# A norm's column products and root rows dealt out between other products, squares summed in three views, and T1 and T2 placed behind the blocks

## The chip, the cores and the metric

The kernel runs on one core of a Trainium2 chip. The metric is the device time of one launch in microseconds (us), the median of the runs. Engines are called as in the profile: PE is TensorE (matrix products), PEld its weight loads, DVE VectorE, ACT ScalarE, POOL GpSimd, SP SyncE (which starts DMAs here).

## What is computed

Two layers on a sequence of 1024 rows of 1024 numbers. Each has a token mixer (layer 0 forgetting attention, layer 1 gated linear attention, GLA) and a dense SwiGLU feed-forward part. Each of the four parts begins with an RMS norm, scaled and shifted by a conditioning vector:

```python
def rms_norm(x, g):
    y = x * rsqrt(mean(x * x, axis=-1, keepdims=True) + EPS)
    return y * g

for i in range(2):
    sh1, sc1, g1, sh2, sc2, g2 = split(silu(c) @ ada_w[i] + ada_b[i], 6)
    h = rms_norm(x, norm1_g[i]) * (1 + sc1) + sh1
    x = x + g1 * (attention(h) if i == 0 else gla(h))
    h = rms_norm(x, norm2_g[i]) * (1 + sc2) + sh2
    gate, up = split(h @ ffn_w_in[i], 2)
    x = x + g2 * ((silu(gate) * up) @ ffn_w_out[i])
return rms_norm(x, final_g)
```

All is float32. The change concerns the norm ahead of the two feed-forward parts and the norm between the layers.

## The kernel before

The activations lie transposed: x is eight tiles `xs[0..7]` of 128 features by 1024 rows, worked on in two halves of 512 rows (`hf` 0 and 1). To keep float32 precision, each factor is split into a high part (cast on ACT, L163) and a low part (subtraction on DVE, L164), and `mm3` (L240) makes three products for each tile of the contraction, high by high (L241), high by low (L242), low by high (L243). They add up in a bank of PSUM.

A norm of a half goes in these steps:

- `SumSq` (L572) squares the tile of each finished feature block m on ACT and adds squares on DVE and POOL (L590) in a tree. With `late=7` the last squares are not added in: four views remain (`roots`, L578), v0, v4, v6 and v7.
- `rms_cols` (L526) sums over the features: for each of four groups of 128 rows and each view, PE makes a product of 128x1 (L531) with a column of ones. These 16 are the column products, into the PSUM tile sp.
- DVE takes mean plus eps (L534), POOL the power -1/2 (L535), into rs.
- `rms_rows` (L539) spreads the result over all partitions by four products of 128x128 with the identity (L543), into rb: the rows.
- The views are scaled by rb and split: for the layer norm in `norm_half` (L549, te and h1h/h1l from L556 on), for the feed-forward part in `second_half` (L1209). There the feed-forward input is kept in blocks of the Strassen kind: B11 and B21 are the first half's, B12 and B22 the second half's (scaling at L1175, low part at L1183), T1 = B12 - B11 and T2 = B22 - B21 are differences (L1217 to L1220; low part of T1 at L1180).

While the second half is normed, PE has work of the first half: in the feed-forward stage the tiles (0,0), (0,1) and then (1,0) of gate and up, each of 8 x 3 products with 512 columns (`plain_tile`, L1330; PSUM tiles p); at the boundary between the layers the value products of GLA (`gv_body`, PSUM tiles gv, 256 columns each), with a split of the small weights w2t and aw on DVE.

The order on an engine is set by a scheduler that simulates a timeline of the program, and by `tc.issue_after(ins)`, which holds what is written in its block behind `ins` in the order only. Each engine runs its own list strictly in this order; waits between engines follow from the data. In before, the columns stand in the program ahead of the first tiles, the scheduler puts one of the 16 between the first products and the other 15 in one burst, and `GK = (2, 6)` holds products k >= 2 of tile (0,1) behind the columns, and those of k >= 6 behind the rows. At the boundary `sp_ins` and `rb_ins` do that for the second value body and the gate products.

The last stretch that the prediction speaks of is the first head of GLA: at00 and at01 are its score tiles (both in PSUM bank b3), atz the masked scores (copy on DVE, L1759), ahl their split, go the products with the values, gr the gate projection, kv the state products.

Of the kernel before, what the change touches and what calls it, by code (L numbers as in the profile page):

```python
# [9 lines left out]
F32 = mybir.dt.float32  # L10
# [4 lines left out]
ALU = mybir.AluOpType  # L15

P = 128
# [36 lines left out]
def trunk(ctx, tc, x, c, ada_w, ada_b, norm1_g, norm2_g, ffn_w_in, ffn_w_out,  # L54
# [171 lines left out]
    class Weights:  # L226
# [7 lines left out]
        def next(self):  # L234
# [2 lines left out]
                self.got.append(f(*a))  # L237
            return self.got.popleft()

    def mm3(ps, ah, al, bh, bl, start, stop):  # L240
        nc.tensor.matmul(ps, ah, bh, start=start, stop=False)  # L241
        nc.tensor.matmul(ps, ah, bl, start=False, stop=False)  # L242
        nc.tensor.matmul(ps, al, bh, start=False, stop=stop)  # L243

    def proj(ps, w, hs, hf):

# [273 lines left out]

    sp_ins, rb_ins = [], []
    LATE1 = 7
    GK = (2, 6)
    SPM, RBM = (3, 4)

    def rms_cols(ss, nm, psr, n=4):  # L526
# [17 lines left out]
        rb_ins.append(last_ins())  # L544
        return rb

    first_half = []

    def norm_half(xs, ss, hs, l, hf, psr, tmp):  # L549

        rb = rms_rows(ss, f"{l}0{hf}", psr)
        gates = [(SPM, sp_ins[-1]), (RBM, last_ins())]
        cs = hsl(hf)
        for k in range(8):
            y = tmp()
            hi, lo = hs[k].hi[:, cs], hs[k].lo[:, cs]  # L556
            if k % 2 == 0:
                nc.vector.scalar_tensor_tensor(y, xs[k][:, cs], acol(l, 0, k), rb, op0=ALU.mult, op1=ALU.mult)
                nc.scalar.activation(hi, y, AF.Identity, bias=mcol(l, 0, k))
                nc.vector.scalar_tensor_tensor(lo, y, mcol(l, 0, k), hi.bitcast(F32),  # L560
                                               op0=ALU.add, op1=ALU.subtract)
            else:
                nc.vector.tensor_mul(y, xs[k][:, cs], rb)
                nc.scalar.activation(y, y, AF.Identity, scale=acol(l, 0, k), bias=mcol(l, 0, k))
                nc.scalar.copy(hi, y)
                nc.gpsimd.tensor_sub(lo, y, hi.bitcast(F32))
        if hf == 0:
            first_half.append(last_of("G"))
        return gates

    class SumSq:


        def __init__(self, v, hf, late):
            w = slice(256 * (hf % 2), 256 * (hf % 2) + 256) if hf > 1 else slice(0, HALF)
            self.v = [v[i][:, w] for i in ((1, 3, 2, 5, 7, 6, 3, 4) if hf else range(8))]
            self.late = late
            self.roots = {0: [self.v[0]], 8: [self.v[0]], 7: [self.v[0], self.v[4], self.v[6], self.v[7]],  # L578
                          5: [self.v[0], self.v[4], self.v[5], self.v[6], self.v[7]]}[self.late]

        def __call__(self, m, xk):
            v = self.v
            nc.scalar.activation(v[m], xk, AF.Square)
            if self.late == 0:
                if m:
                    nc.vector.tensor_add(v[0], v[0], v[m])
                return
            d = 1
            while m & d and m < self.late:
                (nc.gpsimd if d == 1 and m < 4 else nc.vector).tensor_add(v[m - 2 * d + 1], v[m - 2 * d + 1], v[m - d + 1])  # L590
                d *= 2


    fr = deque(fl)
# [545 lines left out]
    def ffn(l, oh, xs, slots, nm, mid, norm_end, each=None):  # L1140
# [55 lines left out]
        last_chunk(4, 4, oh, xs, l, 2, nm, sv, norm)  # L1196
        dump(f"xa{l}", xs)
        sg = opr_["sg"]
        rb = rms_rows(ss1[0], f"{l}11", psr)
        block("B22", H_SL[0:4])  # L1200
        block("B12", H_SL[4:8])
        block("T1", H_SL[8:12])
# [3 lines left out]
        y12, y22 = yv_[:4], yv_[4:]  # L1206
        y11, y21 = ya[:4], ya[4:]

        def second_half():  # L1209
# [6 lines left out]
            for k in range(4):  # L1216
                nc.gpsimd.tensor_sub(y11[k], y12[k], y11[k])  # L1217
                split_t(T1[k], y11[k])
                nc.vector.tensor_sub(y11[k], y22[k], y11[k])
                split_t(T2[k], y11[k], sh(k + 4))  # L1220

        x_sp = tc.dram_tile([8, P, S], F32, name=f"x_sp{l}")
        for k in range(8):
# [100 lines left out]

        pin = Ring(psp, list(pj.q) + list(psr.q))
        gs = [Group(*g) for g in GROUPS]
        second_half()
        wgs = [[[None, None], [None, None]] for _ in range(2)]

        def plain_tile(kind, m, hf, after=()):  # L1330
            wg = wgs[kind]
            ps = pin([P, HALF], F32, f"p{l}")
            for k in range(8):
# [5 lines left out]
                with ExitStack() as es:  # L1339
                    for k_, ins in after:  # L1340
                        if k >= k_:
                            es.enter_context(tc.issue_after(ins))
                    mm3(ps, w.hi[:, k % 4, :], w.lo[:, k % 4, :], hi(t), lo(t), k == 0, k == 7)
            d = gate_view(0, (m, hf))
            if kind == 0:
                nc.scalar.activation(d, ps, AF.Silu)
# [1 line left out]
            nc.vector.tensor_mul(d, d, ps)  # L1348
            hid_done(0, (m, hf))

        plain_tile(0, 0, 0)
        plain_tile(0, 1, 0, ((GK[0], sp_ins[-1]), (GK[1], rb_ins[-1])))
        plain_tile(1, 0, 0, ((0, rb_ins[-1]),))
# [494 lines left out]
    with tc.issue_after(sp_ins[-1]):  # L1848
        vt.append(gv_body(0, wv, 1))
    with tc.issue_after(rb_ins[-1]):  # L1850
        bt = gate_tiles(0)
        a_body(aw, 0, bt)
# [125 lines left out]
```

## Time and profile before

| | |
|---|---|
| runs | 2413.99, 2417.68, 2418.18 us; median 2417.68 us |
| span of the profiled execution | 2415.5 us (the page gives no other time of it) |
| mean granted PE clock | 0.993 |
| PE products | 12342 records |
| DMA | 361.88 MB, mean 150 GB/s |

A row of a timeline is: start, duration, engine, line, operation, output<-inputs, shapes, count, and in brackets the idle time before it and what ended that. Times are us from the start of the span. Matmuls are pipelined: a 512-column product is shown with 0.39 us, though one starts every 0.23. The granted clock is a share of full speed, by stretch.

### The profile page before, as it was taken

What the parts mean: (1) busy time and instruction counts of PE and PEld (TensorE: products, weight loads), DVE (VectorE), ACT (ScalarE), POOL (GpSimd) and SP (SyncE); (2) the same over time, 40 slices, a digit from 0 to 9 for tenths busy, and PEclk for the clock granted to TensorE, in tenths of its full rate; (3) what the DMA queues carried; (4) which work ended last, traced back from release to release, by engine and by line L of the source; (5) the groups of instructions that cost most, each with busy time, mean ns of one, the idle gap of its engine ahead of it and who ended that gap; (6) DMA issues with size and microseconds to landing.
All of it is one profiled execution on the core that took longest, in us unless ns stands there. A gap on an engine that the chain in (4) does not pass through costs nothing.

```text
span 2415.5 us, 36053 instructions
## 1 busy us (share of the span) xinstructions
PE 2373.4 (98%) x12342; PEld 2018.3 (84%) x12342; DVE 1672.9 (69%) x2789; ACT 1191.8 (49%) x2288; POOL 1203.4 (50%) x1071
## 2 busy tenths in 40 slices
PE   7999999999999999999999999999999999999998
PEld 6788888878888888888888888898888888888888
DVE  6577677676687877876787545435586767675787
ACT  4665555675544444445324856654343333345325
POOL 4343344432347878853263646662335656653262
PEclk9999999999999999999999999999999999999999
DMA  9233333123335555457665334434325444347664
GB/s 272 72 106 114 100 111 105 62 97 114 127 103 178 184 172 174 155 187 260 228 201 171 89 110 126 135 124 154 114 85 172 164 133 151 133 174 256 232 202 148
DMA packets 329359, 361.88 MB, mean 150 GB/s; under 512 B 24460, under 2 KB 252968, under 8 KB 329176
## 3 DMA queue, kind: packets, MB, share of 16 engines
q1 hardware_dynamic: 328984, 359.57, 45.4%
q8 instruction: 97, 1.59, 0.3%
q14 instruction: 86, 0.70, 0.1%
q10 hardware_dynamic: 192, 0.02, 0.0%
HBM read 269.25 MB, written 90.24 MB: 149 GB/s over the span
## 4 chain that ended last, share of the span: by engine, by line
PE 82%; DVE 5%; DMA 4%; ACT 3%; issue 2%; POOL 2%; SPq 1%; DVEq 0%; POOLq 0%; ACTq 0%
PE p_b L243 16%; PE p_b L241 16%; PE p_b L242 16%; PE o_b L979 2%; PE t_b L965 2%; PE qk_b L241 2%; PE qk_b L243 2%; PE qk_b L242 2%; PE s_b L934 1%; PE s_b L935 1%; PE gr_b L243 1%; PE gr_b L242 1%; PE gr_b L241 1%; PE vps_b L241 1%; PE vps_b L242 1%
## 5 line engine op out<-in xcount | busy, mean ns | idle before, releaser
L164 DVE TENSOR_TENSOR o_s<-xv_s,o_s 128x512 fp32r<-128x512 f32 (+1 forms) x376 | 341.4, 911 | 78.4 <-ACT o_s L163 77.5
L163 ACT CAST o_s<-xv_s 128x512 fp32r<-128x512 f32 (+1 forms) x376 | 217.8, 587 | 320.3 <-PE p_b L243 254.4
L242 PE MATMUL p_b<-B,o_s 128*128 128x512 f32 x608 | 238.1, 392 | 0.0
L243 PE MATMUL p_b<-B,o_s 128*128 128x512 f32 x608 | 237.7, 391 | 0.0
L241 PE MATMUL p_b<-B,o_s 128*128 128x512 f32 x608 | 236.2, 391 | 0.0
L945 POOL TENSOR_SCALAR lp_s<-lp_s,st 128x128 f32<-128x128 f32 (+7 forms) x128 | 98.1, 771 | 265.7 <-DVE st L944 214.7
L708 POOL TENSOR_TENSOR ex_s<-xv_s,xv_s 128x512 f32<-128x512 f32 (+1 forms) x64 | 89.1, 1393 | 261.5 <-DMA xv_s<-in_ffn_w_in_dram 97.1
L241 PE MATMUL p_b<-T,o_s 128*128 128x512 f32 x480 | 186.7, 389 | 0.0
L242 PE MATMUL p_b<-T,o_s 128*128 128x512 f32 x480 | 186.7, 389 | 0.0
L243 PE MATMUL p_b<-T,o_s 128*128 128x512 f32 x480 | 180.7, 389 | 0.0
L243 PEld LDWEIGHTS p_b<-B,o_s 128*128 128x128 f32 x608 | 114.7, 189 | 23.9
L241 PEld LDWEIGHTS p_b<-B,o_s 128*128 128x128 f32 x608 | 114.7, 189 | 23.8
L242 PEld LDWEIGHTS p_b<-B,o_s 128*128 128x128 f32 x608 | 114.7, 189 | 23.7
L943 ACT ACTIVATE lp_s<-lp_s,st 128x128 f32<-128x128 f32 (+7 forms) x128 | 99.3, 777 | 61.1 <-DVE st L939 58.7
L381 POOL TENSOR_TENSOR ad_s<-ad_s,ad_s 128x512 f32<-128x512 f32 x62 | 89.4, 1442 | 54.0 <-ACT ad_s L379 29.6
L163 ACT CAST pt_s<-t_b 128x512 fp32r<-128x512 f32 (+1 forms) x160 | 79.6, 547 | 73.5 <-PE t_b L965 72.8
L710 POOL TENSOR_TENSOR xv_s<-ex_s,xv_s 128x512 f32<-128x512 f32 (+1 forms) x64 | 84.9, 1327 | 57.3 <-DVE o_s L164 55.1
L1319 DVE TENSOR_TENSOR ex_s<-ex_s,p_b 128x512 f32<-128x512 f32 x140 | 94.0, 680 | 27.0 <-PE p_b L243 26.9
L164 DVE TENSOR_TENSOR pt_s<-t_b,pt_s 128x512 fp32r<-128x512 f32 (+1 forms) x160 | 96.8, 631 | 13.2 <-ACT pt_s L163 12.9
L243 PEld LDWEIGHTS p_b<-T,o_s 128*128 128x128 f32 x480 | 90.1, 188 | 18.7
L241 PEld LDWEIGHTS p_b<-T,o_s 128*128 128x128 f32 x480 | 90.1, 188 | 18.7
L242 PEld LDWEIGHTS p_b<-T,o_s 128*128 128x128 f32 x480 | 90.1, 188 | 18.7
(1952 smaller groups left out, 7505.7 us busy)
## 6 DMA issues: line engine op xcount, KB each, us to landing
xv_s<-in_ffn_w_in_dram SPq DMA_DIRECT2D x176, 256.0 KB, 3.0
hid_B<-x SPq DMA_DIRECT2D x70, 512.0 KB, 2.7
ad_s<-in_ada_w_dram SPq DMA_DIRECT2D x384, 64.0 KB, 1.9
hid_T<-x SPq DMA_DIRECT2D x36, 512.0 KB, 2.8
xv_s<-in_ffn_w_out_dram SPq DMA_DIRECT2D x96, 192.0 KB, 4.1
ada_s<-in_ada_w_dram SPq DMA_DIRECT2D x128, 128.0 KB, 2.6
xv_s<-in_ffn_w_out_dram SPq DMA_DIRECT2D x40, 256.0 KB, 2.8
T2o<-hid_T SPq DMA_DIRECT2D x18, 512.0 KB, 9.0
```

The source lines that it names most:

```text
L163: nc.scalar.copy(hi, src)
L164: nc.vector.tensor_sub(lo, src, hi.bitcast(F32))
L241: nc.tensor.matmul(ps, ah, bh, start=start, stop=False)
L242: nc.tensor.matmul(ps, ah, bl, start=False, stop=False)
L243: nc.tensor.matmul(ps, al, bh, start=False, stop=stop)
L381: nc.gpsimd.tensor_add(acc, acc, raw)
L708: nc.gpsimd.tensor_add(s1, a21, a22)
L710: nc.gpsimd.tensor_sub(a11, s1, a11)
L943: nc.scalar.activation(lp, lp, AF.Exp, bias=mcur, scale=-1.0, accum_out=st[:, qi, 2:3])
L945: nc.gpsimd.tensor_scalar(lp, lp, st[:, qi, 3:4], 1.0, op0=ALU.mult, op1=ALU.mult)
L965: nc.tensor.transpose(tp[:, i, :], lps[qi][:, psl(2 * b + jj)], ident)
L1319: nc.vector.tensor_add(d, d if src is None else dest(G, src), ps)
```

## The change

Three edits, for the second half's norms with `late=7` (the first feed-forward stage, the boundary, and the second feed-forward stage):

1. *Three views.* After the square of m = 5, DVE adds v4 to v0 (L647 of after), and `roots` has three entries. A norm has 12 column products.
2. *Dealing.* `rms_later` returns the norm's steps as functions: the four columns of v0; then four pairs of the other two views, the root, a number of empty steps (8, or 13 at the boundary), and the four rows one by one. They go into the list `between`. Each product of `mm3` now takes one step from it and places it behind itself, and the next product behind the step. In the feed-forward stage v0's columns start at k = 4 of tile (0,0) and the rest at k = 2 of tile (0,1). At the boundary 24 empty steps, then v0's columns, belong to the first value body, the rest to the second.
3. *T1 and T2.* The step that makes T1 and T2 is held behind the last DVE instruction of B22.

The core of the diff:

```diff
+    def product(ps, a, b, start, stop):
+        with ExitStack() as es:
+            if tail:
+                es.enter_context(tc.issue_after(tail.pop()))
+            nc.tensor.matmul(ps, a, b, start=start, stop=stop)
+        if between:
+            f = between.popleft()
+            with tc.issue_after(last_of("P")):
+                if f is not None:
+                    f()
+            tail.append(last_of("P"))
...
-        nc.tensor.matmul(ps, ah, bh, start=start, stop=False)
+        product(ps, ah, bh, start, False)
...
-    GK = (2, 6)
+    GK = 2
...
+    def rms_later(ss, nm, psr, then, gap=8):
...
+        return ([lambda t=t: sums(0, t) for t in range(4)],
+                [lambda t=t: last(t) for t in range(4)] + [root] + [None] * gap
+                + [lambda t=t: row(t) for t in range(4)])
...
-            self.roots = {0: [self.v[0]], 8: [self.v[0]], 7: [self.v[0], self.v[4], self.v[6], self.v[7]],
+            self.roots = {0: [self.v[0]], 8: [self.v[0]], 7: [self.v[0], self.v[6], self.v[7]],
...
+            if self.late == 7 and m == 5:
+                nc.vector.tensor_add(v[0], v[0], v[4])
...
+            with tc.issue_after(last_of("D")):
+                for k in range(4):
+                    nc.gpsimd.tensor_sub(y11[k], y12[k], y11[k])
+                    split_t(T1[k], y11[k])
...
+        small = rms_later(ss1[0], f"{l}11", psr, second_half)
+        plain_tile(0, 0, 0, 4, small[0])
+        plain_tile(0, 1, 0, GK, small[1])
+        with tc.issue_after(rb_ins[-1]):
+            plain_tile(1, 0, 0)
...
+    between.extend([None] * 24 + second_norm[0])
     vt = [gv_body(0, wv, 0)]
+    between.extend(second_norm[1])
+    vt.append(gv_body(0, wv, 1))
```

The lists of the engines show what moves. PE in the first feed-forward stage, before; p0 are the tiles, sp011 the columns, and the views are ss0_s31 (v0), s34 (v4), s32 and s33:

```order
L242 MATMUL p0_b4_1_7662<-B2103_7116,o00001_s20_2_7456 128x512
L243 MATMUL p0_b4_1_7662<-B2103_7116,o00001_s20_2_7456 128x512
L531 MATMUL sp011_b6_3_7489<-ones_74,ss0_s34_7108 128x1
L531 MATMUL sp011_b6_3_7489<-ones_74,ss0_s32_7106 128x1
L531 MATMUL sp011_b6_3_7489<-ones_74,ss0_s33_7107 128x1
L531 MATMUL sp011_b6_3_7489<-ones_74,ss0_s31_7105 128x1
```

PE at the same norm, after, from the last products with B11 on:

```order
L247 MATMUL p0_b4_1_7590<-B1103_7112,o00000_s19_1_7422 128x512 x3
L247 MATMUL p0_b4_1_7590<-B2100_7113,o00001_s20_2_7457 128x512
L569 MATMUL sp011_b6_3_7607<-ones_74,ss0_s31_7105 128x1
L247 MATMUL p0_b4_1_7590<-B2100_7113,o00001_s20_2_7457 128x512
L569 MATMUL sp011_b6_3_7607<-ones_74,ss0_s31_7105 128x1
L247 MATMUL p0_b4_1_7590<-B2100_7113,o00001_s20_2_7457 128x512
```

The burst began behind the tile's last product; v0's columns now begin in the middle of the tile, behind its 20th product in the list (tile (0,1)'s first ones, which stand among them, counted in). DVE there, after; x0 are the updates of x, L644 is the add of square 5, L647 the new one:

```order
L1130 SCALAR_TENSOR_TENSOR x0_6_6212<-fo1461p_b2_15_7460,modc_167,x0_6_6212 128x512
L1130 SCALAR_TENSOR_TENSOR x0_7_6213<-fo1471p_b3_16_7475,modc_167,x0_7_6213 128x512
L644 TENSOR_TENSOR ss0_s34_7108<-ss0_s34_7108 128x512
L647 TENSOR_TENSOR ss0_s31_7105<-ss0_s31_7105,ss0_s34_7108 128x512
L578 TENSOR_SCALAR rs011_7645<-sp011_b6_3_7607 128x4
```

The add is new; the rows ahead of it stand in before in the same order. DVE at the boundary, after; se0_s40 is v4 and se0_s36 v0, w2t and aw are small weights:

```order
L1130 SCALAR_TENSOR_TENSOR x0_7_6213<-f0e11871p_b5_16_12888,modc_167,x0_7_6213 128x512
L644 TENSOR_TENSOR se0_s40_12504<-se0_s40_12504 128x512
L164 TENSOR_TENSOR w2t_12927<-w2raw_s18_93_12924,w2t_12927 16x512 x2
L164 TENSOR_TENSOR aw_s21_85_12938<-aw_s16_94_12936,aw_s21_85_12938 128x8x16
L647 TENSOR_TENSOR se0_s36_12501<-se0_s36_12501,se0_s40_12504 128x512
L164 TENSOR_TENSOR gvt00_s53_1_13033<-gv00_b0_1_12962,gvt00_s53_1_13033 128x512
```

The new add stands behind the splits of w2t and aw. PE there, after, at the end of the first value tile (24 products) and the start of the second:

```order
L247 MATMUL gv00_b0_1_12962<-wv1024_4h_s45_83_12880,h1l7_12692 128x256
L247 MATMUL gv00_b0_1_12962<-wv1024_0h_s23_81_12855,h1h0_12677 128x256
L569 MATMUL sp101_b3_1_12988<-ones_74,se0_s36_12501 128x1
L247 MATMUL gv00_b0_1_12962<-wv1024_0l_s24_82_12856,h1h0_12677 128x256
L569 MATMUL sp101_b3_1_12988<-ones_74,se0_s36_12501 128x1
```

The first column, which reads v0, stands behind the 26th gv product (one product of a third tile is among them); in before, all but one of the columns stood behind the 48th. PE in the first head of GLA, before, where the products with the split scores ahl00 begin:

```order
L241 MATMUL gr010_b1_2_13720<-h1h5_12690,w2176_h_s46_92_13406 128x512
L242 MATMUL gr010_b1_2_13720<-h1l5_12691,w2176_h_s46_92_13406 128x512
L241 MATMUL go000_b5_1_13677<-gvt00_s53_1_13083,ahl00_s52_1_13637 128x256
L242 MATMUL go000_b5_1_13677<-gvt00_s53_1_13083,ahl00_s52_1_13637 128x256
L241 MATMUL go001_b6_2_13740<-gvt01_s25_2_13143,ahl00_s52_1_13637 128x256
```

And after:

```order
L247 MATMUL at01_b3_2_13785<-gq00h_s32_1_13506,kih0_s28_1_13408 128x128
L247 MATMUL at01_b3_2_13785<-gq00l_s33_2_13507,kih0_s28_1_13408 128x128
L247 MATMUL at01_b3_2_13785<-gq00h_s32_1_13506,kil0_s29_2_13409 128x128
L247 MATMUL gr010_b1_2_13714<-h1h7_12691,w2176_h_s46_92_13400 128x512
L247 MATMUL go000_b5_1_13671<-gvt00_s53_1_13033,ahl00_s52_1_13631 128x256 x2
```

The twelve products of at01 and four more of gr010 now stand ahead of go000. On DVE in the feed-forward stages, three low parts of T1 that stood among those of B22 now stand behind the last of B22; the subtractions on POOL keep their order.

More of the change, by code (lines that the diff above doesn't have):

```diff
@@ L1326, in ffn, with plain_tile @@
         gs = [Group(*g) for g in GROUPS]
[L1327 removed]
         wgs = [[[None, None], [None, None]] for _ in range(2)]
[L1330 removed]
+        def plain_tile(kind, m, hf, at=None, small=()):
             wg = wgs[kind]
@@ L1338, in plain_tile @@
                 t = (b["B12"] + B22)[k] if hf else (B11 + B21)[k]
[L1339 to L1343, printed above, removed]
+                if k == at:
+                    between.extend(small)
+                mm3(ps, w.hi[:, k % 4, :], w.lo[:, k % 4, :], hi(t), lo(t), k == 0, k == 7)
             d = gate_view(0, (m, hf))
@@ L1846, in trunk @@
         aw = feed.next()
+    between.extend([None] * 24 + second_norm[0])
     vt = [gv_body(0, wv, 0)]
-    with tc.issue_after(sp_ins[-1]):
-        vt.append(gv_body(0, wv, 1))
+    between.extend(second_norm[1])
+    vt.append(gv_body(0, wv, 1))
+    assert not between
     with tc.issue_after(rb_ins[-1]):
```

53 lines of the change are left out of this document (37 added, 16 removed).

## The prediction

> **What bounds the kernel now.** I read the busy shares first, then the chain of work that ended last, then the stretches that the change touches.
>
> ```profile
> PE 2373.4 (98%) x12342; PEld 2018.3 (84%) x12342; DVE 1672.9 (69%) x2789; ACT 1191.8 (49%) x2288; POOL 1203.4 (50%) x1071
> PE 82%; DVE 5%; DMA 4%; ACT 3%; issue 2%; POOL 2%; SPq 1%; DVEq 0%; POOLq 0%; ACTq 0%
> 669.14 3.24 PE sp_b L531 x30
> 676.74 0.99 PE rb_b L543 x8
> ```
>
> TensorE is busy for 98% of the span and is 82% of the chain, so the time is the number of its instructions, their pace, and its few waits. The third and fourth rows are pieces of the chain: the burst of 15 column products (two records each, so x30) and the four root rows of the second half's norm in the first feed-forward stage. They are on the path. Two other norms have the same pair of pieces: the boundary between the layers, and the second feed-forward stage.
>
> A look at these stretches by windows shows a second cost. The columns are: stretch, its length, busy time and instructions on PE, PEld, DVE, ACT, POOL, then the granted clock, DMA share and GB/s.
>
> ```profile
> 668.90:672.20 3.30, 3.30 (x32) 3.26 (x30) 0.00 (x0) 0.95 (x2) 1.39 (x2) 1.00 0.36 142
> 673.20:676.50 3.30, 3.30 (x9) 2.51 (x9) 0.00 (x0) 0.00 (x0) 0.48 (x1) 0.53 0.00 0
> 1322.00:1325.00 3.00, 3.00 (x15) 3.00 (x16) 0.16 (x1) 0.00 (x0) 1.02 (x1) 0.50 1.20 302
> 1762.30:1765.60 3.30, 3.30 (x10) 2.55 (x9) 0.00 (x0) 0.00 (x0) 0.28 (x1) 0.50 0.00 0
> 1393.60:1403.80 10.20, 9.71 (x35) 8.46 (x34) 4.64 (x9) 6.12 (x12) 6.58 (x7) 0.50 0.52 154
> ```
>
> In the first row the array runs the burst at a clock of 1.00. Right behind it, for about 3.3 us, the clock is half, and nine products stand where some fifteen would. The same half-speed stretch follows the bursts at the boundary and in the second feed-forward stage. A half-speed stretch of 3.30 us at 0.53 or 0.50 costs 3.30 x 0.47 to 3.30 x 0.50, so 1.6 us; the one at the boundary 3.00 x 0.50 = 1.5. So a burst costs its own 3.4 us and 1.5 to 1.6 behind it, though PE had no pause. The fifth row, half speed for 10.2 us, follows a real wait in the first head of GLA, to which I come below.
>
> **The change part by part, columns.** Four views become three, so each norm has 12 columns for 16.
>
> ```profile
> 662.38 0.28 PE L531 MATMUL sp_b<-ones,ss_s 128*128 128x1 f32 x2
> 668.98 3.40 PE L531 MATMUL sp_b<-ones,ss_s 128*128 128x1 f32 x30
> ```
>
> 15 columns take 3.40 us, 0.227 each, and the single one between two products takes 0.28 with its overlap. Dealing columns out therefore neither saves nor costs anything by itself: I take 0.23 each, and 4 x 0.23 = 0.92 us saved per norm. The rows (0.99 for four in the chain) are four before and four after, and I cost their dealing at nothing.
>
> **The half-speed stretches.** If no 3.4 us on end consist of single columns, the stretches behind the bursts should go: -1.6 us at each feed-forward norm, -1.5 at the boundary. What replaces them depends on new pauses.
>
> The Trainium skill ("TensorE: Matmul & The Clock Gate", Part 1: The HAM clock gate) says that a free-running window of about 3.4 us decides the clock, and that an idle window brings half speed; its section "Why this matters for your kernels" asks for no PE pause above some 3 us. The rows agree with the length, but not with the pause: here half speed follows a window in which PE was busy throughout, with products one column wide. By the page's rule taken literally the two feed-forward norms after the change are safe, with pauses of 2 us, and the sum below would be 1.6 us lower.
>
> **The added add on DVE, feed-forward norms.** The saved view is paid with an add, v0 += v4, on DVE behind the add of square 5. All columns of v0 wait for it, and these stand early on PE. These are DVE and PE at the first feed-forward norm:
>
> ```profile
> 665.88 0.75 DVE L1074 SCALAR_TENSOR_TENSOR x<-fo1461p_b,modc,x 128x512 f32<-128x512 f32 x1
> 666.54 0.74 DVE L1074 SCALAR_TENSOR_TENSOR x<-fo1471p_b,modc,x 128x512 f32<-128x512 f32 x1
> 667.20 0.68 DVE L590 TENSOR_TENSOR ss_s<-ss_s 128x512 f32<-128x512 f32 x1
> 661.93 0.62 PE L241 MATMUL p_b<-B,o_s 128*128 128x512 f32 x2
> 665.57 0.39 PE L241 MATMUL p_b<-B,o_s 128*128 128x512 f32 x1
> 665.80 0.39 PE L242 MATMUL p_b<-B,o_s 128*128 128x512 f32 x1
> ```
>
> The last two rows give a product every 0.23 us. In the order of after, the first column stands behind 20 products of the tile that starts at 661.93, so PE is there at 661.93 + 20 x 0.227 = 666.5. The new add can start when the add at 667.20 is through, at about 667.8, and takes 0.68 as that one does: 668.5. PE waits 2.0 us, with the rest of the tile queued behind the column. In the second feed-forward stage the order is the same, and so I expect the same. The norm's balance: -0.92 - 1.6 + 2.0 = -0.5 us. But the pause of 2.0 and four columns just behind it lie in about one 3.4 us window, which may then be as empty as one full of columns. Whether it is depends on where the window falls; I give it one in two and 1.6 us. Two norms: -1.0 with no such stretch, +2.2 with two; I take one, **+0.6**.
>
> **The boundary.** Here the new add stands behind other DVE work.
>
> ```profile
> 1317.96 0.67 DVE L590 TENSOR_TENSOR se_s<-se_s 128x512 f32<-128x512 f32 x1
> 1318.55 1.39 DVE L164 TENSOR_TENSOR w2t<-w2raw_s,w2t 16x512 fp32r<-16x512 f32 x2
> 1319.97 0.29 DVE L164 TENSOR_TENSOR aw_s<-aw_s,aw_s 128x128 fp32r<-128x128 f32 x1
> 1315.31 0.28 PE L241 MATMUL gv_b<-wv_0h_s,h1h 128*128 128x256 f32 x1
> 1315.43 0.28 PE L242 MATMUL gv_b<-wv_0l_s,h1h 128*128 128x256 f32 x1
> 1318.68 3.63 PE L531 MATMUL sp_b<-ones,se_s 128*128 128x1 f32 x30 [0.33 <-DVE se_s L590]
> ```
>
> Before, PE works through two value tiles and then waits 0.33 us for the squares. After, the add follows both splits of w2t and that of aw: it starts at 1319.97 + 0.29 = 1320.26 and ends 0.68 later, 1320.9. The first column stands behind 26 of the gv products; the 25th and 26th are those at 1315.31 and 1315.43, less the early column of before, so PE arrives at 1315.5. It waits **5.4 us**, with 23 products of the second value tile queued behind the column that need nothing from it. That is longer than a window, so half speed follows; at least part of it falls into the pause itself, where it costs nothing. Between none (0) and one and a half stretches (2.6) I take 1.4. Sum: -0.92 - 1.5 - 0.33 + 5.4 + 1.4 = **+4.0** (+2.6 to +5.2).
>
> **T1 and T2 behind the blocks.** The DVE subtractions and low parts of T1 and T2 move behind the last low part of B22.
>
> ```profile
> 692.39 0.74 DVE L1183 SCALAR_TENSOR_TENSOR B<-yb_s,modc,B 128x512 fp32r<-128x512 f32 x1
> 677.76 2.72 DVE L1175 SCALAR_TENSOR_TENSOR yb_s<-x,amul,rb_b 128x512 f32<-128x512 f32 x4 [5.18 <-PE rb_b L543]
> 685.52 0.68 DVE L1180 TENSOR_TENSOR T<-ya_s,T 128x512 fp32r<-128x512 f32 x1
> ```
>
> In the order of before three low parts of T1 (0.68 each) stand ahead of that last low part of B22, which so could come some 2 us sooner, while the later rows delay the views by about 0.9. No PE product of the stage waits for these parts, so their coming sooner is worth nothing; and their coming later is covered by the products of B12 and B22 that stand ahead of T1's. If that cover were gone, a whole sub and split, 1.4 us, would show. I take 0.
>
> **GLA's first head.** The order of after differs there too: the products of at01 and four more of the gr tile now stand ahead of go000.
>
> ```profile
> 1389.80 0.39 PE L242 MATMUL gr_b<-h1l,w_h_s 128*128 128x512 f32 x1
> 1392.15 0.39 PE L241 MATMUL go_b<-gvt_s,ahl_s 128*128 128x256 f32 x1 [1.97 <-ACT ahl_s L163]
> 1390.74 0.71 DVE L1759 COPY_PREDICATED atz_s<-tri,at_b 128x512 f32<-128x512 int32 x1
> ```
>
> Before, PE stands for about 2 us until ahl is cast. After, it has four more products (0.9 us, to 1390.9), then at01, whose bank is free when the copy at 1390.74 ends, 1391.45: a wait of 0.5. At01's 12 products cover the rest. So 1.5 us are saved, and the emptiest window before the half-speed stretch of 10.2 us (loss 10.2 x 0.5 less 0.5 idle, so 4.9) is no longer that empty. But at full speed PE would catch up with the decay and state steps of the other engines and wait there. Bounds: 0 if the relative times shift, -6.4 if all goes; I take **-3.5**.
>
> **Sum.** +0.6 + 4.0 - 3.5 = +1.1 us on the profiled execution, whose span is 2415.5. The page gives no time outside the span; the median of the runs, 2417.7, is 2.2 above that span. I put the difference on the median: **2418.8 us**, no change. About 0.2%, 4.8 us, is what a measurement of this kernel can tell from none.
>
> **The rivals.**
> *Slower.* DVE's add is the bound at all three norms, and each pause brings half speed, while GLA keeps its wait: +2.2 + 5.2 + 0 = +7.4, 2425.1. For it: the two pauses are certain by the order, and the slow stretches of before came without any pause at all. Against it: the reordered GLA products need only a copy that ends 0.7 us before ahl's split. It decides from a pause at the boundary of about 5 us with GLA unchanged. Chance 0.22.
>
> *GLA in full.* The half-speed stretch there goes altogether and neither feed-forward norm has one: -1.0 + 4.0 - 6.4 = -3.4, 2414.3; with no new stretch at the boundary either, 2412.9. For it: the gap of 1.97 is the one real pause ahead of that stretch. Against it: other engines' rows in it. Chance 0.2, a third of it beyond 0.2%.
>
> *Faster, the deal as the words have it.* DVE comes to the add before PE comes to the column, so that no pause arises: 3 x 0.92 + 2 x 1.6 + 1.5 + 0.33 = -7.8, 2409.9. For it: the costs removed are plain rows of the chain. Against it: on DVE the add cannot run before 667.8, and 1320.3 at the boundary, by rows of the trace. It needs DVE 2 and 5 us ahead of where it was. Chance 0.13.
>
> **How the numbers follow.** The forecast keeps 0.45: from -0.5 us (no half speed at the feed-forward norms) to +4.6 (GLA saves nothing). Faster by over 0.2%: 0.13 and a third of 0.2, so 0.2. Slower: 0.22 and 0.03 for the forecast's upper end with a dearer boundary, 0.25. No change: 0.55. The range goes from 2410 (the third rival) to 2425 (the first).
>
> **What would show it.** Right: a PE wait of about 2 us on the first column of the feed-forward norms and of 5 to 6 at the boundary, released by the new add on DVE; no half speed behind the last columns; 12 columns; go000 without a wait of 2 us. Wrong: first columns that do not wait (then the third rival), or half speed behind the dealt columns although PE never pauses (then the column count, not the burst, sets the clock), or a wait for B22's or T1's parts (then the cover that I cost at nothing is not there).

## The result, and the profile after

The change made the kernel slower by 0.4%: median 2426.0 us (2423.7 to 2428.8, 5 runs) for 2416.2 us before (2414.0 to 2418.2, 5 runs), a ratio of 1.004 with a 95% interval of 1.0028 to 1.0052. I had forecast 2418.8 us, no change, +1.1 us on the 2417.7 of three runs of before; the time lies above my range, and the difference between the medians is +9.8.

The page of after, busy times:

```profile
PE 2373.4 (98%) x12318; PEld 2019.0 (83%) x12318; DVE 1677.4 (69%) x2792; ACT 1191.8 (49%) x2288; POOL 1201.1 (49%) x1071
```

PE's busy time is the same to a tenth of a microsecond, 24 records (12 columns) fewer notwithstanding, since half speed stretches the rest; the span is 2426.7 us for 2415.5. Three of the waits of PE (line waited for: us in total, times, longest):

```profile
PE sp_b L569 <- DVE ss_s L647: 7.1, 2, 4.0
PE sp_b L569 <- DVE se_s L647: 5.6, 1, 5.6
...
PE go_b L247 <- DVE ahl_s L164: 0.5, 1, 0.5
```

The first two are the waits of v0's first columns for the added add, at the two feed-forward norms together and at the boundary: 12.7 us that before did not have. The third is the wait for ahl in GLA's first head, 0.5 where before had 1.97. The half-speed stretches by windows (columns as in the prediction):

```profile
672.90:679.50 6.60, 6.26 (x19) 5.37 (x20) 0.19 (x1) 0.00 (x0) 1.32 (x1) 0.52 0.11 42
1324.90:1335.00 10.10, 7.30 (x36) 7.34 (x37) 2.59 (x4) 1.45 (x3) 1.18 (x2) 0.52 0.81 217
1765.20:1771.80 6.60, 5.39 (x17) 4.70 (x18) 1.07 (x1) 0.00 (x0) 0.52 (x1) 0.52 0.13 46
1393.00:1407.00 14.00, 13.24 (x76) 11.23 (x75) 9.39 (x9) 10.85 (x17) 12.16 (x12) 1.00 0.54 157
```

Before, half speed lasted some 3.4 us at each norm. Now it lasts twice that at the feed-forward norms and three times at the boundary, partly under PE's wait. GLA's first head (last row) is at a clock of 1.00.

To see where the time went I compared the starts of the same PE products in both traces. The differences by stretch, after minus before, are +3.5 us ahead of the first feed-forward norm, where the change has done nothing yet; **+4.2** at that norm; **+5.9** at the boundary; **-5.7** in GLA's first head; **+4.7** at the second feed-forward norm; -1.1 and -0.4 in places that the change doesn't touch. The four bold ones make +9.1, near the 9.8 between the medians. The +3.5 and the two small ones belong to the single execution: runs below have -1.7 to +3.4 at the same place ahead of the first norm. The profiled execution of the change, and below that of `early`, is the slowest of its runs and that of `four` the fastest, so their sums of stretches differ from their medians by some 3 to 4 us.

The added add at the first feed-forward norm, on DVE and beside it POOL and PE:

```profile
670.75 0.68 DVE L644 TENSOR_TENSOR ss_s<-ss_s 128x512 f32<-128x512 f32 x1
671.46 1.63 DVE L647 TENSOR_TENSOR ss_s<-ss_s,ss_s 128x512 f32<-128x512 f32 x1
...
670.73 1.82 POOL L764 TENSOR_TENSOR ex_s<-xv_s,xv_s 128x512 f32<-128x512 f32 x1 [14.01 <-DMA xv_s<-in_ffn_w_in_dram]
672.62 1.60 POOL L765 TENSOR_TENSOR xv_s<-xv_s 128x512 f32<-128x512 f32 x1
...
665.47 4.70 PE L247 MATMUL p_b<-B,o_s 128*128 128x512 f32 x20
673.24 0.56 PE L569 MATMUL sp_b<-ones,ss_s 128*128 128x1 f32 x2 [3.08 <-DVE ss_s L647]
```

Twenty products, then the column, as the order said, 3.5 us later in this execution than in the one of before. But the add takes 1.63 us, not 0.68, beside a POOL addition that is under way, and it ends 0.54 after that has ended (670.73 + 1.82 = 672.55). In the second feed-forward stage both adds are slow:

```profile
1762.97 1.63 DVE L644 TENSOR_TENSOR ss_s<-ss_s 128x512 f32<-128x512 f32 x1
1764.63 1.63 DVE L647 TENSOR_TENSOR ss_s<-ss_s,ss_s 128x512 f32<-128x512 f32 x1
...
1762.78 1.27 POOL L764 TENSOR_TENSOR ex_s<-xv_s,xv_s 128x512 f32<-128x512 f32 x1 [13.84 <-DMA xv_s<-in_ffn_w_in_dram]
1764.13 1.59 POOL L765 TENSOR_TENSOR xv_s<-xv_s 128x512 f32<-128x512 f32 x1
...
1766.41 0.56 PE L569 MATMUL sp_b<-ones,ss_s 128*128 128x1 f32 x2 [4.02 <-DVE ss_s L647]
```

### The profile page after: what moved, and what is told of

Read it like the earlier page. It is cut to its first block, busy times and chain, and to the rows that moved or that the text cites. A ratio compares the mean times of both kernels' runs of the same rounds, so it can differ in the third digit from the quotient of the medians.

```text
span 2426.7 us, 36033 instructions
## 1 busy us (share of the span) xinstructions
PE 2373.4 (98%) x12318; PEld 2019.0 (83%) x12318; DVE 1677.4 (69%) x2792; ACT 1191.8 (49%) x2288; POOL 1201.1 (49%) x1071
## 4 chain that ended last, share of the span: by engine, by line
PE 79%; DVE 8%; DMA 4%; ACT 3%; issue 3%; POOL 2%; SPq 1%; DVEq 0%; POOLq 0%; ACTq 0%
PE p_b L247 43%; PE qk_b L247 5%; PE vps_b L247 3%; PE gv_b L247 3%; PE gr_b L247 3%; PE o_b L1035 2%; PE t_b L1021 2%; PE s_b L990 1%; PE s_b L991 1%; DVE o_s L164 1%; PE go_b L247 1%; PE gk_b L247 1%; POOL x L1570 1%; DVE x L1568 1%; DMA xv_s<-in_ffn_w_out_dram 1%
## 5 line engine op out<-in xcount | busy, mean ns | idle before, releaser
L247 PE MATMUL p_b<-B,o_s 128*128 128x512 f32 x1824 | 443.9, 393 | 0.5 <-DVE B L1239 0.5
L247 PE MATMUL p_b<-T,o_s 128*128 128x512 f32 x1440 | 345.6, 389 | 0.0
L995 DVE CUSTOM_DVE_ANT_0 lp_s<-s_b,cum_s 128x512 f32<-128x512 f32 (+3 forms) x128 | 72.7, 570 | 40.6 <-PE t_b L1021 21.6
L1035 PE MATMUL o_b<-pt_s,v_s 128*128 128x256 f32 x512 | 94.0, 294 | 5.8 <-DVE pt_s L164 3.4
L209 POOL TENSOR_TENSOR w_l_s<-w__s,w_h_s 128x256 fp32r<-128x256 f32 x120 | 89.2, 776 | 20.6 <-ACT w_h_s L206 20.6
L776 POOL TENSOR_TENSOR xv_s<-xv_s,xv_s 128x512 f32<-128x512 f32 x40 | 55.8, 1394 | 84.3 <-issue 65.2
L765 POOL TENSOR_TENSOR xv_s<-xv_s 128x512 f32<-128x512 f32 (+1 forms) x64 | 92.5, 1445 | 4.6
L1552 DVE TENSOR_TENSOR x<-x,p_b 128x512 f32<-128x512 f32 x112 | 74.8, 679 | 27.1 <-PE p_b L247 22.5
L247 PE MATMUL qk_b<-h0h,w_h_s 128*128 128x512 f32 x224 | 92.0, 411 | 0.0
L1236 DVE TENSOR_TENSOR x<-sg_s,x 128x512 fp32r<-128x512 f32 x58 | 69.0, 1190 | 32.0 <-ACT x L1235 30.8
```

Source lines behind the costliest of these rows:

```text
L209: (nc.gpsimd if i < lo_p else nc.vector).tensor_sub(lo[:, cs], rw[:, cs], hi[:, cs].bitcast(F32))
L247: nc.tensor.matmul(ps, a, b, start=start, stop=stop)
L765: nc.gpsimd.tensor_sub(a21, a11, a21)
L1035: nc.tensor.matmul(ops, lv, pts[b][:, hl, 2 * jj:2 * jj + 2, :], start=j == 0 and hl == 0, stop=False)
```

## The experiments

Theory W, of the first batch, is that the loss is PE's wait for the added add and the half speed it brings. Where I speak of a stretch's gain or loss, it is the same comparison of starts, against the one profiled execution of before. That execution had an unusually long half-speed stretch in GLA (10.2 us; another kernel with its order there had 3.4), so GLA's figures lean towards a gain by 0.5 to 1.3 us. At the boundary, too, `tmove` and `gla` below, which leave it as before has it, come out at -1.1 and -0.9: a gain of 1 us there is no more than that.

**Four views, dealt out** (`four`): the added add taken out again.

```diff
-            self.roots = {0: [self.v[0]], 8: [self.v[0]], 7: [self.v[0], self.v[6], self.v[7]],
+            self.roots = {0: [self.v[0]], 8: [self.v[0]], 7: [self.v[0], self.v[4], self.v[6], self.v[7]],
-            if self.late == 7 and m == 5:
-                nc.vector.tensor_add(v[0], v[0], v[4])
```

> The change with its four views kept: no added add on DVE, 16 columns, still dealt out at the same places; T1 and T2 as in the change. Theory W (the loss is PE's wait for the added add at v0's first column, and the half speed that the wait and the sparse columns behind it bring): v0 is ready long before its columns, so no wait on them at the three norms, no half-speed stretch there, and GLA's first head without its 10.24 us stretch, as in the change; against before, -1.6 x 2 - 1.5 - 0.3 at the norms and about -5.5 in GLA, near 2406 us. Rival D (dealing single columns between products itself makes the windows sparse and drops the clock, wherever they stand): half speed behind the columns as in the change, some 3 us at each norm, no waits; 2415 to 2422 us.

Measured: 2409.4 us, ratio 0.9968 (0.9955 to 0.998). PE has no wait on a column, and the norms give -1.0, -1.0 and -1.0, GLA -7.7. This is its stretch with 16 columns dealt out, four of them single, then threes:

```profile
666.89 0.28 PE L569 MATMUL sp_b<-ones,ss_s 128*128 128x1 f32 x2
...
670.31 0.72 PE L569 MATMUL sp_b<-ones,ss_s 128*128 128x1 f32 x6
...
671.21 0.72 PE L569 MATMUL sp_b<-ones,ss_s 128*128 128x1 f32 x6
...
668.00:674.00 6.00, 6.00 (x41) 5.45 (x41) 0.46 (x2) 2.25 (x3) 2.73 (x2) 1.00 0.43 170
1320.40:1323.60 3.20, 3.20 (x18) 3.20 (x17) 0.04 (x1) 0.21 (x1) 1.02 (x1) 0.55 1.22 304
```

The clock stays at 1.00 through the columns; only the boundary, where three columns stand to one product of 256, has half speed. Taking back this one edit, the summing into three views with its add, recovers more than the whole loss: theory W holds for the loss. D shows at the boundary alone, where half speed came though PE had been busy for all of the 3.4 us ahead of it (1316.5 to 1319.9).

**Three views, columns later** (`late`).

```diff
-        small = rms_later(ss1[0], f"{l}11", psr, second_half)
-        plain_tile(0, 0, 0, 4, small[0])
-        plain_tile(0, 1, 0, GK, small[1])
+        small = rms_later(ss1[0], f"{l}11", psr, second_half, 5)
+        plain_tile(0, 0, 0)
+        plain_tile(0, 1, 0, GK, small[0] + small[1])
...
-    between.extend([None] * 24 + second_norm[0])
...
-    between.extend(second_norm[1])
+    between.extend([None] * 20 + second_norm[0] + second_norm[1])
```

> The change with its three views, but all 12 columns later: at both feed-forward norms from k = 2 of tile (0,1) on, with 5 empty steps instead of 8 before the rows; at the boundary 20 products into the second value body. Theory W: PE comes to the first column at about the time when the add is through; waits under 1 us at each norm, no half speed, 12 columns for 16: -0.9 x 3 - 1.6 x 2 - 1.8 at the norms and -5.5 in GLA, some 1 to 3 us given back by a later root; 2404 to 2408 us. Rival S (the third view's add, which ran beside a POOL operation and took 1.6 us, delays the norm's chain wherever the columns stand): PE waits somewhere else for the same time, 2420 us or more. Rival D: half speed remains, 2415 to 2420 us.

Measured: 2416.5 us, ratio 0.9995 (0.9983 to 1.0008): some 10 us better than the change, but no better than before, and 9 above what I expected. The first feed-forward norm is at -0.9 and the boundary at -1.1, with the same three views and the same add (1.67 us at the feed-forward norm), so the place of the columns, not the add itself, made the loss there. The second feed-forward norm is at +2.3: a wait of 0.6 and 12 columns close together brought 6.8 us of half speed there, and none at the first norm, where both are the same. GLA gave -1.7 only.

**Three views in before** (`views`): the burst as before, 12 columns, and the add.

```diff
-            self.roots = {0: [self.v[0]], 8: [self.v[0]], 7: [self.v[0], self.v[4], self.v[6], self.v[7]],
+            self.roots = {0: [self.v[0]], 8: [self.v[0]], 7: [self.v[0], self.v[6], self.v[7]],
+            if self.late == 7 and m == 5:
+                nc.vector.tensor_add(v[0], v[0], v[4])
```

> The kernel before with three views alone: the added add, 12 columns for 16, burst and rows in blocks as before, T1 and T2 as before. Theory W: at the feed-forward norms the burst stands some 7 us behind the place where the change has v0's first column, so PE waits under 1 us for the add; at the boundary the burst stands at 1318.4 and the add ends at 1320.9, a wait of 2 to 3 us. Saved 3 x 0.9 us; half speed behind a burst of 11 columns in some places still. 2413 to 2418 us, no change. Rival S: the add alone costs several us, 2420 us or more.

Measured: 2422.9 us, ratio 1.0025 (1.0016 to 1.0034), a miss: +1.7, +3.4 and +1.2 at the norms, +1.0 in GLA. The waits, as PE's sums show, are about as W had them at the boundary, but longer at the second feed-forward norm (1.9), where the slow adds of the trace above come again, and half speed lasts 6.8 us at the first norm and at the boundary:

```profile
PE sp_b L531 <- DVE ss_s L593: 2.7, 2, 1.9
PE sp_b L531 <- DVE se_s L593: 2.7, 1, 2.7
```

So the third view costs by its wait even with the burst at its late place; 12 columns for 16 don't pay for it.

**T1 and T2 alone** (`tmove`): the third edit, in before.

```diff
+            with tc.issue_after(last_of("D")):
                 for k in range(4):
                     nc.gpsimd.tensor_sub(y11[k], y12[k], y11[k])
...
```

> The kernel before with T1 and T2 behind the low parts of the blocks and nothing else. I costed this at nothing: 2416 us within 1.5, half-speed stretches as in before, no PE wait for T1 or T2. Rival: the later T parts are late for PE at the first product with T1, or the low parts of B22 that come sooner end waits that the trace of before does not show; over 2 us either way.

Measured: 2416.4 us, ratio 1.0001 (0.9991 to 1.0011). It is worth nothing. Its second feed-forward norm has 6.8 us of half speed and +1.6 all the same, with before's burst and no wait: so much can come of where the windows fall.

**The add earlier** (`early`): the columns stay, DVE's queue is changed.

```diff
+                held[:] = [last_of("D")]
+            if m == 7:
+                held.clear()
...
+                with ExitStack() as es:
+                    if held:
+                        es.enter_context(tc.issue_after(held[0]))
                     nc.vector.scalar_tensor_tensor(xs[m][:, cs], ps, mcol(l, j, m), xs[m][:, cs],
...
```

> The change with the added add earlier on DVE: the updates of x for blocks 6 and 7 are held behind it, so that at the feed-forward norms it stands 1.3 us sooner (0.66 for each update) and ahead of the POOL operation beside which it took 1.6 us, and at the boundary ahead of those updates and the split of aw. Columns stay where the change has them. GLA's first head has at01 behind go, as before. Theory W: the waits at v0's column fall from 3.1 and 4.0 to about 1 us, from 5.6 to about 2 or 3; little half speed at the feed-forward norms, so there about -1 to -2 us each against before, boundary +1 to +3, GLA 0: 2414 to 2418 us. Rival S (the third view costs by its add wherever it stands): 2420 us or more.

Measured: 2420.6 us, ratio 1.0021 (1.0012 to 1.003). Both feed-forward norms go from +4.2 and +4.7 to -0.9 and -0.9, with no half speed. DVE, POOL and PE at the first of them:

```profile
669.24 0.69 DVE L646 TENSOR_TENSOR ss_s<-ss_s 128x512 f32<-128x512 f32 x1
669.96 0.69 DVE L649 TENSOR_TENSOR ss_s<-ss_s,ss_s 128x512 f32<-128x512 f32 x1
...
670.53 1.29 POOL L769 TENSOR_TENSOR ex_s<-xv_s,xv_s 128x512 f32<-128x512 f32 x1 [14.01 <-DMA xv_s<-in_ffn_w_in_dram]
...
670.80 0.35 PE L569 MATMUL sp_b<-ones,ss_s 128*128 128x1 f32 x2 [0.82 <-DVE ss_s L649]
```

1.3 us sooner in the queue, the add is through before POOL's addition has taken hold, takes 0.69 again, and PE waits 0.8. At the boundary the scheduler still put it behind the splits of w2t; PE waits 4.9 us there, and that norm stays at +5.8, which more than makes up the 4.5 us of the median above before. The expectation was right on the feed-forward norms and wrong on the boundary; the time is as rival S had it, but not for its reason, since the add costs little at the two norms where it stands earlier.

**GLA's order in before** (`gla`): at01 written ahead of the go products.

```diff
+        pre = []
         for g in range(2):
-            ahl = intra(g)
+            ahl = pre.pop() if pre else intra(g)
             yield 1.3
+            if g == 0 and h == 0:
+                pre.append(intra(1))
```

> The kernel before with one thing moved: in GLA's first head the score products at01 are written, and so stand, ahead of the first go products, as the scheduler had put them in the change and in the run with four views. Theory G (a good part of what the change gained and lost is this order, which the edit does not ask for): PE waits well under 1 us for ahl, no 10 us half-speed stretch at 1393, norms as in before; 5 to 7 us faster than before, about 2409.5. Rival: the gain in GLA came with the other times of the engines at the boundary; then the order alone gives 0 to 2 us, 2414 to 2416.

Measured: 2415.8 us, ratio 0.9998 (0.9988 to 1.0008). Theory G falls in this form, and the time is the rival's. The wait has only moved from go to at01, whose bank is free when DVE has copied atz:

```profile
1391.49 0.30 PE L241 MATMUL at_b<-gq00h_s,kih_s 128*128 128x128 f32 x1 [2.07 <-DVE atz_s L1759]
```

**Feed-forward norms alone** (`ffn_only`): four views, the boundary's norm as before.

```diff
-        if hf:
-            second_norm.extend(rms_later(ss, f"{l}0{hf}", psr,
-                                         lambda rb: norm_views(rb, xs, hs, l, hf, tmp), 13))
-            return
...
-    between.extend(second_norm[1])
-    vt.append(gv_body(0, wv, 1))
+    with tc.issue_after(sp_ins[-1]):
+        vt.append(gv_body(0, wv, 1))
```

> Four views, dealt out at the two feed-forward norms only; the boundary's norm in a burst as before; at01 behind part of go. Theory W with G: -1.0 us at each feed-forward norm as in the run with four views, 0 at the boundary, and nothing like its 7 us in GLA; 2413 to 2415 us. Rival: the run with four views was fast by the dealing at the norms themselves; then this one is at 2410 or under.

Measured: 2416.4 us, ratio 0.9998 (0.9989 to 1.0006); slower than I expected. -1.0 at the second norm, but +0.6 at the first, where half speed came behind the columns though PE never waited; +1.4 at the boundary, and GLA -2.5. So threes of columns can bring half speed with no wait: D has a part.

**The boundary spread** (`spread`): four views, the boundary's later columns and rows one behind every second product.

```diff
-    between.extend(second_norm[1])
+    sn = second_norm[1]
+    between.extend([f for g in sn[:12] for f in (None, g)] + [sn[12]] + [None] * 8
+                   + [f for g in sn[-4:] for f in (None, g)])
...
```

> The run with four views, with the boundary's 12 later columns and its rows dealt one behind every second product of 256 columns, where it had three behind one. GLA's first head has the order of before here. If a window is slow when the share of it with columns moving through the array is under about a third (0.24 in that run's boundary window), the boundary has no half speed now and gains 1 to 1.5 us more than that run's 1.0 there; norms -1.0 and -1.0; GLA 0; 2411 to 2414 us. Rival (one-column products of any density bring half speed): the boundary as in that run, 2414 us or more.

Measured: 2416.5 us, ratio 0.9997 (0.9987 to 1.0007). The boundary is at -1.9 with no half speed, as expected; the first feed-forward norm, whose threes were left, has half speed again and +0.6, and GLA gives -2.5 only. The median is a miss by 2 us.

**v0's columns in one block** (`block`): the change with this alone.

```diff
-        return ([lambda t=t: sums(0, t) for t in range(4)],
+        return ([lambda: [sums(0, t) for t in range(4)]],
```

> The change with v0's four columns in one block instead of one behind each of four products, at all three norms; the added add and so the wait stay. In the change, half speed lasts two windows (6.8 us) at the feed-forward norms; my reading is that the first comes of the wait, and the second of four single columns alternating with four products at half speed, which fill a whole window. Then it lasts one window (3.4 us) here at the feed-forward norms, and each is about 1.5 us better than in the change: +2.5 to +3.3 us for +4.2 and +4.7. Rival (the wait alone sets the length): still 6.8 us, +4 to +5 each.

Measured: 2422.9 us, ratio 1.0035 (1.0021 to 1.0048). The first feed-forward norm has one window of half speed and +2.9, as I expected; the second has two and +4.1, as the rival had it, with the same wait of 3.1 us:

```profile
668.03 1.02 PE L569 MATMUL sp_b<-ones,ss_s 128*128 128x1 f32 x8 [3.07 <-DVE ss_s L647]
1758.98 1.84 PE L569 MATMUL sp_b<-ones,ss_s 128*128 128x1 f32 x8 [3.08 <-DVE ss_s L647]
...
670.00:673.30 3.30, 3.30 (x12) 2.56 (x10) 0.00 (x0) 0.00 (x0) 0.00 (x0) 0.60 0.00 0
1758.60:1761.90 3.30, 2.92 (x11) 2.76 (x12) 0.23 (x1) 0.00 (x0) 1.36 (x1) 0.50 0.27 102
1762.00:1765.00 3.00, 3.00 (x8) 2.29 (x8) 0.00 (x0) 0.00 (x0) 0.00 (x0) 0.52 0.00 0
```

In the second, half speed sets in while PE still waits (the wait fell into two windows), so two windows were sparse. My reading, that the alternation makes the second window, is not needed where the wait itself lies so; whether it has a part elsewhere stays open.

**GLA's order back** (`gla_back`): four views with at01 held behind the first go products.

```diff
+            with ExitStack() as es:
+                if g and h == 0:
+                    es.enter_context(tc.issue_after(go_ins[0]))
+                ahl = intra(g)
...
```

> The run with four views with GLA's first head put back in the order of before: at01 behind the first go products. If the order there made that run's gain of 7.7 us in GLA, PE waits about 2 us for ahl again and GLA gives only 0 to 2.5 us, 2414 to 2416 us in all. Rival (the gain came of the earlier boundary, not of the order; for it stands that the same order put into the kernel before gave 0.3 us): 2409 to 2411 us as in that run.

Measured: 2410.9 us, ratio 0.998 (0.9971 to 0.9989): GLA gives -6.4 still, the time that the rival named. In the order of this run 46 products of gr stand between at00 and go; in the change and in `four` it is 34 and at01; in before 30. So it is not at01. Nor is it an earlier boundary, as that rival says: in the change the boundary is 5.9 us late, and GLA gave -5.7. What the three have in common is more work ahead of go that needs nothing from DVE. ahl is ready 11 to 13 us after at00 begins, and PE comes to go after 11.4 in before, having waited, and after 12.6 and 13.8 in `four` and here, not having waited:

```profile
1395.41 0.88 PE L247 MATMUL go_b<-gvt_s,ahl_s 128*128 128x256 f32 x6
1399.81 0.52 PE L247 MATMUL go_b<-gvt_s,ahl_s 128*128 128x256 f32 x3
```

No run changed that count alone, so this cause is argued from the three orders and not shown. `spread` had no wait on ahl either and gained only 2.5: PE waited 2.5 us for the state (kv) and 1.3 for gr further on.

**All columns single** (`singles`, and `singles_gl` with at01 ahead of go): four views, at the feed-forward norms one column behind each product from the start of tile (0,1), the boundary as in `spread`.

```diff
-        small = rms_later(ss1[0], f"{l}11", psr, second_half)
+        small = rms_later(ss1[0], f"{l}11", psr, second_half, 7, True)
...
-        plain_tile(0, 1, 0, GK, small[1])
+        plain_tile(0, 1, 0, 0, small[1])
```

> Four views, every column single: at the feed-forward norms the 12 later ones one behind each product from the start of tile (0,1), at the boundary one behind every second product. Where three columns stood behind one product at the first feed-forward norm, half speed came in two of four runs, at a share of 0.33 and 0.35 of the window with columns moving, and not at 0.43. With one column to a product of 512 the share is about 0.47 and half speed should not come: -1.0 us at both feed-forward norms, -1.9 at the boundary. GLA's first head has at01 behind go, 0 to -2.5: 2410 to 2413 us. Rival (half speed is chance near the norms, whatever the dealing): one of the three norms has half speed again.

> The same with at01 written ahead of go in GLA's first head. If the order there helps where the boundary is early, 2408 to 2410 us, the fastest of all; if the order gives nothing by itself, as in the kernel before, 2410 to 2413 us.

Measured: 2413.1 us, ratio 0.9989 (0.998 to 0.9998), and 2413.6, ratio 0.999 (0.9981 to 0.9999). No half speed at any of the three norms in either, as expected, with -0.8, +0.4, -0.8. The boundary lost its gain (PE waits later for what comes behind the later root), and GLA gave -3.7 and -4.2, with the wait on ahl back (2.2 and 3.1 us). The order written by hand gave nothing here either. `four`, at 2409.4 us, is the fastest of all and beats both kernels; its lead over `singles` is mostly GLA's.

## Why the prediction was wrong

*The mechanism was right, its sizes were not.* The step that failed first is that the new add "**takes 0.68 as that one does**". It started in time, but took 1.63 us beside POOL's addition of two tiles. In the second stage the add ahead of it was held up too. The waits were 3.1 and 4.0 us for my 2.0. The rows to see it were there in before:

```profile
667.27 1.75 POOL L708 TENSOR_TENSOR ex_s<-xv_s,xv_s 128x512 f32<-128x512 f32 x1 [14.10 <-DMA xv_s<-in_ffn_w_in_dram]
...
1756.78 1.28 POOL L708 TENSOR_TENSOR ex_s<-xv_s,xv_s 128x512 f32<-128x512 f32 x1 [14.70 <-DMA xv_s<-in_ffn_w_in_dram]
```

POOL's sums of weights wait for a DMA and begin at this very place, and the L590 add (667.20 in the prediction's rows) just got in ahead of them; an add behind it could not. I never read POOL's rows there, since POOL is busy for half of the span only. `early` shows it by removing it: 0.69 again. A page of the Trainium skill that I had not applied, "SBUF — State Buffer", in its section "Who interferes with whom", says that a DVE operation with two inputs in SBUF and a GpSimd operation that reads SBUF lock each other out, whoever comes second waiting for the whole instruction. The rows agree: 0.69 ahead of POOL's, 1.63 behind its start.

*"One in two and 1.6 us" for half speed* failed next. Two windows fell at each feed-forward norm, 6.8 us, and three at the boundary, 10.2 us, each time from before the end of the wait. By PE's rows from the first column on, four columns and 11 products took 6.3 us at the first norm (673.24 to 679.54), where 15 x 0.227 = 3.4 would do, and 5.9 at the second; at the boundary four columns and 23 products of 256 took 6.8 us, where 4 x 0.224 + 23 x 0.12 = 3.7 would do. So half speed cost 2.9, 2.5 and 3.1, for my 0.8, 0.8 and 1.4. I had left out that a wait of 3 to 5 us can reach over two windows, so that PE comes out of it at half speed and one more sparse window follows (`block` has it at its second norm, and not at its first). In sum this is the larger miss: 5.5 us, to 3.1 for the waits of the two feed-forward norms.

*The sums with the measured sizes:* at the first feed-forward norm -0.92 - 1.6 + 3.1 + 2.9 = +3.5, and some 0.6 more from a step that I had costed at nothing: "**the later rows delay the views by about 0.9**". PE now waits for them, at a low part of B12:

```profile
692.66 23.65 PE L247 MATMUL p_b<-B,o_s 128*128 128x512 f32 x103 [0.24 <-DVE B L1239]
```

The 0.6 is read off `four`, which has the same 0.24 and -1.0 where I expected the full half-speed gain of 1.6. The record of a product of 512 (0.39) overlaps the next start (0.23), so the row understates the wait, which is up to 0.4; the last 0.2 is not shown. That makes +4.1 in all for a measured +4.2, and at the second norm -0.92 - 1.6 + 4.0 + 2.5 + 0.6 = +4.6 for +4.7. At the boundary -0.92 - 1.5 - 0.33 + 5.58 + 3.1 = +5.9 for a measured +5.9. My wait there, 5.4, was right within 0.2 us, and my 4.0 low by the half speed alone. But the wait was right in part by luck: DVE came to its work there 0.9 us sooner against PE than in before, and the splits of w2t took 2.33 us for the 1.39 of the prediction's row (2.33 to 2.36 in twelve of the fourteen traces, 1.38 in `views`). POOL's subtractions were through ahead of them in before (the first row) and under way in the change:

```profile
1314.98 2.84 POOL L209 TENSOR_TENSOR w_l_s<-w__s,w_h_s 128x256 fp32r<-128x256 f32 x4
...
1322.42 3.66 POOL L209 TENSOR_TENSOR w_l_s<-w__s,w_h_s 128x256 fp32r<-128x256 f32 x4
...
1324.29 2.33 DVE L164 TENSOR_TENSOR w2t<-w2raw_s,w2t 16x512 fp32r<-16x512 f32 x2
```

It is the same meeting of DVE and POOL as at the feed-forward norms: the splits end 0.54 us after POOL (1322.42 + 3.66 = 1326.08).

*GLA:* -3.5 forecast, -5.7 measured, inside my bounds (0 to -6.4). What I gave as the cause, at01 as cover, is wrong in part: at01 waits for the same copy. By the orders the gr products ahead of go are the cover, which no run tested alone.

*T1 and T2:* 0 forecast, 0 measured (`tmove`).

*The rivals.* "Slower" came, by its mechanism at the norms and at +9.8 for its 7.4, but with GLA's gain, which it denied; so its price for the norms, 2.2 + 5.2 = 7.4, was half of the measured 14.8. I should have seen that its prices at the norms had a common cause, the added add and the wait for it, and that a range up to 2425 held only the cheap case of it. "Faster, the deal as the words have it" is what `four` is, at the feed-forward norms: there the dealing alone gave 1 us each, without the 0.92 of the third view, not 2 to 3.

The Trainium skill's rule on the clock ("TensorE: Matmul & The Clock Gate", Part 1: The HAM clock gate, and "Why this matters for your kernels") ties half speed to an idle window, or a pause above some 3 us. The pauses of 3.1, 4.0 and 5.6 us fit the second. `ffn_only` and `spread` had half speed with PE busy throughout, so the rule is too mild here.

## What to carry to other kernels

An addition that saves a few products has to be costed at the place where it stands in its engine's queue, with what the other engines do there at the same moment, not by its median duration; and then by who waits for it. A step dealt in between products needs its inputs ready at its first piece, since the in-order engine stops for that piece with all the work behind it. And when a scheduler orders the program, a change at one place moves others: GLA's first head, which no line of the change names, gave 5.7 us where the three norms lost 14.8, and gave most of the gain of `four`, the fastest version.

## What the runs showed of the hardware

- A DVE addition with both inputs in SBUF (128x512, float32) that starts while a POOL addition runs ends about 0.55 us after that has ended: 1.63 us for 0.68. The same add 1.3 us sooner took 0.69. Twice it was POOL's addition that took longer, 1.75 us in before and 1.82 in the change for 1.27 to 1.29 in the other rows shown: it began within 0.1 us of a DVE addition that took its 0.68. Two splits of 16x512 took 1.39 us with POOL through and 2.33 beside its subtractions.
- Half speed needs no pause of PE. I worked out, from the starts and widths of PE's products, the share of each 3.4 us window in which columns move through the array at full rate (0.107 us for 256 columns, the difference between the spacings of 0.227 for 512 and 0.12 for 256). Next to the three norms, in all runs, half speed followed every window of 0.37 or less that had begun at full clock (0.26 to 0.29 behind the two feed-forward bursts and in the change; 0.33 and 0.35 at threes of columns), and none of 0.40 or more. The share isn't all of it: near 570 us windows of 0.32 to 0.37 kept full clock in six runs. One column behind each 512-column product (0.46 to 0.54) brought no half speed in either run that had it; three sometimes did.
- A 128x1 product costs 0.22 to 0.23 us of PE between products of 512, in a row or dealt out: in `four` a product with three columns takes 0.90 us (670.31 to 671.21), 0.227 + 3 x 0.224.
